# Two output blocks of the merged mixer formed in turn, and the retention heads' rows scaled and turned two heads at a time

## The chip, the cores and the metric

The kernel runs on one core of one Trainium2 chip. The metric is the device time of one execution in microseconds (us), as the median of several runs. The engines are named as in the profile: PE (TensorE, matmuls), PEld (its weight loads), DVE (VectorE), ACT (ScalarE), POOL (GpSimd) and SP (SyncE, which here issues DMAs). "L206" is line 206 of the kernel before.

## The reference

One decoder layer over S = 256 tokens of width D = 2048, all in float32, depth and batch 1. Shortened to what is computed:

```python
hn = rmsnorm(h, norm_mix_w)
q, k, v, g_ret, xr, yr, g_a, g_b = split(hn @ w_in)
q = rotary(q, positions); k = rotary(k, positions) * RET_QK_DIM ** -0.5
ret = head_groupnorm(chunkwise_retention(q, k, v), ret_gn_w)        # 8 heads, 256 wide each
ret_out = silu(g_ret) * ret
xr = causal_dwconv(xr, rnn_conv_w, rnn_conv_b)                      # 4 taps
rnn_out = gelu(yr) * rg_lru(xr, ...)
merged = sigmoid(g_a) * (ret_out @ w_proj_ret) + sigmoid(g_b) * (rnn_out @ w_proj_rnn)
h = h + merged @ w_mix_out
h = h + memory_cross_attention(rmsnorm(h), rmsnorm(mem), xa_w_q, xa_w_k, xa_w_v, xa_w_o)
h = h + conv_gated_ffn(rmsnorm(h), ffn_w_up, ffn_conv_w, ffn_conv_b, ffn_w_down)
return rmsnorm(h, final_norm_w)
```

## The kernel before

**Products.** A float32 product is made of three matmuls in a 32-bit format of lower precision (fp32r): each operand is split into a high part and the remainder, and high x high, low x high and high x low are added up in PSUM. All weights are read once. The host lays them out as a stream of chunks in the order of use; a chunk is 1 MB, four k-tiles of 128 rows by 512 columns. SP loads it into one of three raw buffers (L244), ScalarE makes its high parts (`hi`, L269), VectorE the remainders (`lo`, L270), two parts of two k-tiles each. There are six buffers for parts, three chunks' worth, and `prefetch` works two chunks ahead of the one that PE uses. A block of 512 output columns has 16 k-tiles, thus four chunks, and a chunk of the kind used here has 24 matmuls of 512 columns on PE (`mm`, L206; two token halves by four k-tiles by three products).

**Order.** `weight_plan` lists the blocks in the order in which the program takes them; `weight_stream` lists the chunks in the order in which they lie in memory, and an assertion holds the program to it. At the start, two blocks are already mixed chunk by chunk. At the end, three of the last blocks of `ffn_w_down` are streamed with the last chunk of each behind all the others. `steps_n` is a generator that does one chunk of a block at each step, and `ended` runs one to its end. The accumulators come from a PSUM pool of three. The order of instructions on each engine is fixed when the program is built: a scheduler places them by priorities and by its own estimate of times. Each engine then executes its list in order and waits where an operand isn't there yet.

**Work beside the products.** `later(n, fn)` puts a function off until n + 1 more chunks have been used. `by_dma(rows, then, wait)` turns a block of 256 token rows by 512 columns: ScalarE copies its two 16-bit halves into planes (`pl`, L380, two copies), SP issues two DMA transposes (L382, `pt`), and, put off by `wait`, ScalarE joins the halves again (`f`, L391, two copies) and `then` is called with the result.

**Places that matter here.**

- Retention: for a group of four heads, `normalise` (called when the fourth head's output is there) subtracts the mean and multiplies by the gate on VectorE, and scales by the inverse deviation on ScalarE (L653, eight instructions: four heads by two token halves) into two `rows` tiles of two heads each; both are then turned by `by_dma` with waits 2 and 3. The words go to the list `words`, which `split_head` uses ahead of `w_proj_ret`.
- Behind the second group come the RG-LRU blocks: products for `xr` and `yr`. `turned_rows` scales a product's rows (L404, VectorE) and turns them; `conv_x` then applies the conv, its first tap on ScalarE (L763) and three more for each of four tiles on VectorE (L765, 12 instructions).
- Merge: `gated` forms the gated block `m` (L806); block `b` of the merged activations is added up (L820) and turned by `by_dma` with the default wait of 1; `turn_merged` splits it into operands (`s`, L423 on ScalarE, L424 on VectorE).
- `residual("w_mix_out", ...)` takes the four blocks of `w_mix_out` one after the other. Each is added to the residual rows (`nat`, L835), squared for the norm (L850) and turned; `turn` splits it with the norm's weights (`split_cols`, L446 on ScalarE and L447 on VectorE). Before block 1, `memory_steps` squares the rows of the memory (L488, eight instructions); before block 3, it puts off the splits of the memory's pairs, which `xa_w_k` uses next.

Of the kernel before, what the change touches and what calls it, by code (L numbers as in the profile page):

```python
# [17 lines left out]
P = 128  # L18
D = 2048
S = 256  # L20
NT = D // P
HEADS = 8
DK = 128
DV = 256
# [4 lines left out]
BW = 512  # L29
KC = 4  # L30
# [37 lines left out]
def weight_plan():  # L68

    plan = []  # L70
    for g in range(2):
        for c in (O_Q, O_K):
            plan += [("w_in", 0, NT, c + g * BW), ("w_in", 0, NT, O_V + g * 1024 + (c == O_K) * BW)]
        plan += [("w_in", 0, NT, O_G + g * 1024 + b * BW) for b in range(2)]
    for b in range(4):
        plan += [("w_in", 0, NT, c + b * BW) for c in (O_XR, O_YR)]
    for c, w in ((O_GB, "w_proj_rnn"), (O_GA, "w_proj_ret")):
        for b in range(4):
            plan += [("w_in", 0, NT, c + b * BW), (w, 0, NT, b * BW)]
    plan += [("w_mix_out", 0, NT, b * BW) for b in range(4)]  # L80
    plan += [(w, 0, NT, b * BW) for b in range(4) for w in ("xa_w_k", "xa_w_q")]
    plan += [(w, 0, NT, b * BW) for w in ("xa_w_v", "xa_w_o") for b in range(4)]
    for kind, *a in ff_plan():
        if kind == "down":
            plan += [("ffn_w_down", a[0] * BW, 4 * a[1], b * BW) for b in range(4)]
        else:
            plan.append(("ffn_w_up", 0, NT, (0 if kind == "gate" else FF) + a[0] * BW))
    return plan
# [15 lines left out]
def pieces(i, nk):  # L104

    sizes = EARLY if i < 2 else [KC] * (nk // KC)
    return [(sum(sizes[:j]), n) for j, n in enumerate(sizes)]


def weight_stream():  # L110

    out = [
        [(w, row + k * P, n, c) for k, n in pieces(i, nk)]
        for i, (w, row, nk, c) in enumerate(weight_plan())
    ]
    out[:2] = [[one for pair in zip(*out[:2]) for one in pair]]
    out[-4:-1] = [[c for o in out[-4:-1] for c in o[:-1]] + [o[-1] for o in out[-4:-1]]]
    return [one for chunks in out for one in chunks]


# [10 lines left out]
def hybrid_layer(  # L131
# [16 lines left out]
    act, dve, pe, pool, sp = nc.scalar, nc.vector, nc.tensor, nc.gpsimd, nc.sync  # L148
# [11 lines left out]
    def nm(s):  # L160
        count[0] += 1
        return f"{s}_{count[0]}"

    def big(shape, dt=F32, s="b"):
        return bp.tile(shape, dt, tag="big", name=nm(s))
# [4 lines left out]
    def acc():  # L170
        return pm.tile([P, 2, BW], F32, tag="acc", name=nm("acc"))
# [108 lines left out]
    def later(n, fn):  # L280

        pending.append((step[0] + n + 1, fn))
# [18 lines left out]
    def ended(steps):  # L301

        for a in steps:
            pass
        return a
# [41 lines left out]
    def steps_n(w, row, st, nk, col):  # L347

        a = acc()
        for k0, n, parts in chunks(nk, w, row, col):  # L350
            for tt in range(2):
                for kk in range(n):
                    k = k0 + kk
                    hi, lo = (t[:, kk % KH, :] for t in parts[kk // KH])
                    products_n(a[:, tt, :], st[k // 2][:, k % 2, :], hi, lo, tt, k == 0, k == nk - 1)
                if tt == 0 and isinstance(st, Pairs):
                    st[min(NT, k0 + 3 * n) // 2 - 1]
            yield a

    def gemm_n(*args):  # L360
        return ended(steps_n(*args))
# [10 lines left out]
    def by_dma(rows, then, wait=1):  # L372


        planes = big([P, 2, 2, BW], U16, s="pl")
        turned_ = big([P, 2, 4, S], U16, s="pt")
        words = rows.bitcast(U16).rearrange("p t (n h) -> p h t n", h=2)
        with tc.high_priority(FREE):
            for h in range(2):
                act.copy(planes[:, :, h, :], words[:, h])  # L380
        for tt in range(2):
            sp.dma_start_transpose(  # L382
                out=turned_.rearrange("p h f s -> p (h f) s")[:, :, tt * P : (tt + 1) * P],
                in_=planes[:, tt].rearrange("p h n -> p (h n)"),
            )

        def join():
            f = big([P, 4, S], s="f")
            halves_ = f.bitcast(U16).rearrange("p f (s h) -> p h f s", h=2)
            for h in range(2):  # L390
                act.copy(halves_[:, h], turned_[:, h])  # L391
            then(f)

        later(wait, join)
# [97 lines left out]
    def sums():  # L492
        return sp_.tile([P, 2, 4], F32, tag="ss0", name=nm("ss"))
# [103 lines left out]
    ret, words = [], []  # L597
# [5 lines left out]
    def retain(g, qr, kr, vs, dec, gates):  # L603

        stats = sp_.tile([P, 8, 2], F32, tag="mv", name=nm("mv"))
        raws = []

        def scores(hh):
            sc = small((P, 384))
            k, q = kr[hh // 2], qr[hh // 2]  # L610
            product(sc[:, 0:S], halves(k, hh % 2, slice(0, P)), halves(q, hh % 2), True, True)
            late = slice(P, S)
            product(sc[:, S : S + P], halves(k, hh % 2, late), halves(q, hh % 2, late), True, True)
            pr_ = tp.tile([P, 384], F32, tag="pret", bufs=2, name=nm("pret"))
            dve.tensor_tensor(out=pr_[:, 0:S], in0=sc[:, 0:S], in1=dec[:, hh, :], op=ALU.mult)
            dve.tensor_tensor(out=pr_[:, S:384], in0=sc[:, S:384], in1=dec[:, hh, 0:P], op=ALU.mult)
            phi, plo = (tp.tile([P, 384], F32R, tag="tmp", name=nm("ps")) for _ in range(2))
            act.copy(phi, pr_)
            dve.tensor_tensor(out=plo, in0=pr_, in1=phi.bitcast(F32), op=ALU.subtract)
            later(0, lambda: values(hh, phi, plo))  # L620

        def values(hh, phi, plo):
            vc = slice((hh % 2) * DV, (hh % 2 + 1) * DV)
            v0, v1 = ([t[:, tt, vc] for t in vs[hh // 2]] for tt in range(2))
            p0, p1, p2 = ([t[:, c * P : (c + 1) * P] for t in (phi, plo)] for c in range(3))
            ro = small()
            product(ro[:, 0, :], p0, v0, True, True)
            product(ro[:, 1, :], p1, v0, True, False)
            product(ro[:, 1, :], p2, v1, False, True)
            bn = sp_.tile([P, 2, 6], F32, tag="bn", name=nm("bn"))  # L630
            rc = tmp("rc")
            act.copy(rc, ro)
            for tt in range(2):
                dve.bn_stats(out=bn[:, tt, :], in_=rc[:, tt, :])
                dve.bn_aggr(out=stats[:, 2 * hh + tt, :], in_=bn[:, tt, :])
            raws.append(rc)
            if hh == 3:
                normalise()

        def normalise():  # L640
            rows = [big([P, 2, BW], s="rows") for _ in range(2)]
            rstd = rsqrt_small(stats[:, :, 1], 8, 1.0, GN_EPS).rearrange("p (h t) -> p h t", t=2)
            for tt in range(2):
                dve.tensor_scalar_mul(rstd[:, :, tt], rstd[:, :, tt], rs0[:, tt : tt + 1])
            for hh in range(4):
                for tt in range(2):
                    y = raws[hh][:, tt, :]
                    dve.scalar_tensor_tensor(
                        out=y, in0=y, scalar=stats[:, 2 * hh + tt, 0:1],
                        in1=gates[hh // 2][:, tt, (hh % 2) * DV : (hh % 2 + 1) * DV],  # L650
                        op0=ALU.subtract, op1=ALU.mult,
                    )
                    act.mul(rows[hh // 2][:, tt, (hh % 2) * DV : (hh % 2 + 1) * DV], y, rstd[:, hh, tt : tt + 1])  # L653
            for i, r in enumerate(rows):
                by_dma(r, words.append, 2 + i)

        for hh in range(4):
            later(hh, lambda hh=hh: scores(hh))

    for g in range(2):  # L660
        dec = big([P, 4, S], s="dec")
        vs, turned = [], ([], [])
        for b, o in enumerate((O_Q, O_K)):
# [6 lines left out]
            if b == 1:  # L670
                sp.dma_start(
                    out=dec,
# [145 lines left out]
    for b in range(4):  # L818
        m = gated(O_GA, "w_proj_ret", ret, b, big([P, 2, BW], s="m"))
        dve.tensor_add(m, m, mb[b])  # L820
        by_dma(m, turn_merged)


    hrow = [load_rows(x, c) for c in range(4)]
# [3 lines left out]
    def residual(w, st, out, wcol, steps=None):  # L828

        ss = sums()  # L830
        for b in range(4):
            if steps:
                steps(b)
            h = hrow[b]
            dve.tensor_add(h, h, gemm_n(w, 0, st, NT, b * BW))  # L835
            squares(h, ss, b)
            by_dma(hrow[b], lambda f, b=b: turn(f, b, out, wcol))
        return ss
# [209 lines left out]
    for kind, b, *n in ff_plan():  # L1048
# [6 lines left out]
        else:  # L1055
            final = b + n[0] == NF // 4
            if final:
                wfin = []
                for i in range(2):
                    t = big([P, 2, BW], s="wf")  # L1060
                    sp.dma_start(
                        out=t.rearrange("p a n -> p (a n)"),
# [37 lines left out]
```

## Time and profile before

| what | value |
|---|---|
| median of three runs | 2025.03 us |
| the three runs | 2021.9, 2025.03, 2025.69 us |
| the profiled execution, its own time | 2022.28 us |
| its span from the first to the last instruction | 2020.5 us |
| mean granted clock of PE | 0.996 of full |
| instructions | 23630 |
| read from memory | 388.46 MB, 193 GB/s over the span |

The profile shows one execution. Its page gives for each engine the busy time, its share of the span and the number of instructions; groups of instructions by line, with the mean duration of one and what ended the idle time before them; and the chain of work that ended last. The waits list the idle time of an engine by line, with what it waited for: in all, times, longest. In a timeline, a line has start, duration, engine, line, operation, the tile written and those read, shapes and count, and in brackets the idle time before it and what ended that. In a table of windows, a line has the window and its length, then the busy time of PE, PEld, DVE, ACT and POOL with the instructions, then the clock granted to PE (PEclk, 1.00 is full speed), the busy share of the DMA engines and GB/s. Busy time of adjacent instructions overlaps a little, so that sums can exceed the window.

### The profile page before, as it was taken

What the parts mean: (1) busy time and instruction counts of PE and PEld (TensorE: products, weight loads), DVE (VectorE), ACT (ScalarE), POOL (GpSimd) and SP (SyncE); (2) the same over time, 40 slices, a digit from 0 to 9 for tenths busy, and PEclk for the clock granted to TensorE, in tenths of its full rate; (3) what the DMA queues carried; (4) which work ended last, traced back from release to release, by engine and by line L of the source; (5) the groups of instructions that cost most, each with busy time, mean ns of one, the idle gap of its engine ahead of it and who ended that gap; (6) DMA issues with size and microseconds to landing.
All of it is one profiled execution on the core that took longest, in us unless ns stands there. A gap on an engine that the chain in (4) does not pass through costs nothing.

```text
span 2020.5 us, 23630 instructions
## 1 busy us (share of the span) xinstructions
PE 2002.3 (99%) x9060; PEld 1666.2 (82%) x9060; DVE 1264.3 (63%) x1563; ACT 1246.0 (62%) x1502; POOL 7.7 (0%) x12
## 2 busy tenths in 40 slices
PE   9999999999999999999999999999999999999998
PEld 7888888888888888788888888888888888888887
DVE  5856756888645555456555554567675577664675
ACT  6546547989434555478666556666774566644763
POOL 0000000000000000000000000000000000000000
PEclk9999999999999999999999999999999999999999
DMA  8665656665555566777766546667666566655663
GB/s 304 225 210 173 234 199 192 228 213 188 208 188 190 197 204 214 259 225 242 219 198 204 182 167 208 209 189 218 228 203 232 193 195 214 227 215 198 210 228 125
DMA packets 185153, 421.99 MB, mean 209 GB/s; under 512 B 127440, under 2 KB 132176, under 8 KB 139984
## 3 DMA queue, kind: packets, MB, share of 16 engines
q1 hardware_dynamic: 183520, 417.85, 62.2%
q10 hardware_dynamic: 1520, 2.63, 0.4%
q8 instruction: 71, 1.16, 0.2%
q14 instruction: 42, 0.34, 0.1%
HBM read 388.46 MB, written 2.10 MB: 193 GB/s over the span
## 4 chain that ended last, share of the span: by engine, by line
PE 97%; ACT 1%; DVE 1%; DMA 1%; issue 1%; SPq 0%; POOL 0%; POOLq 0%; DVEq 0%; ACTq 0%
PE acc L206 94%; PE sm L206 3%; DMA raw<-in_wall 1%; DVE lo L270 0%; ACT f L391 0%; DVE xr L765 0%; ACT pl L380 0%; ACT rows L653 0%; ACT hi L269 0%; POOL ro L507 0%; PE sm L209 0%; SPq L244 0%; DVE s L447 0%; ACT nat L1034 0%; DVE rows L404 0%
## 5 line engine op out<-in xcount | busy, mean ns | idle before, releaser
L206 PE MATMUL acc<-hi,s 128*128 128x512 f32 (+1 forms) x5680 | 1741.6, 388 | 4.2 <-ACT s L423 4.0
L270 DVE TENSOR_TENSOR lo<-raw,hi 128x1024 fp32r<-128x1024 f32 (+1 forms) x714 | 861.1, 1220 | 662.4 <-ACT hi L269 636.5
L206 PEld LDWEIGHTS acc<-hi,s 128*128 128x128 f32 x5680 | 1062.5, 188 | 222.1 <-ACT s L423 4.5
L206 PE MATMUL acc<-lo,s 128*128 128x512 f32 (+1 forms) x2840 | 1100.8, 388 | 2.0 <-DVE lo L270 2.0
L269 ACT CAST hi<-raw 128x1024 fp32r<-128x1024 f32 (+1 forms) x712 | 736.0, 1051 | 535.4 <-PE acc L206 466.7
L206 PEld LDWEIGHTS acc<-lo,s 128*128 128x128 f32 x2840 | 533.7, 188 | 111.6 <-DVE lo L270 2.7
L391 ACT COPY f<-pt 128x1024 uint16<-128x1024 uint16 x114 | 146.5, 1350 | 68.8 <-DMA pt<-pl 68.6
L380 ACT COPY pl<-rows 128x1024 uint16<-128x1024 uint16 x90 | 89.8, 1046 | 66.1 <-DVE rows L404 58.2
L404 DVE TENSOR_SCALAR rows<-acc,ro 128x512 f32<-128x512 f32 x68 | 47.8, 747 | 2.4 <-PE acc L206 2.4
L957 DVE SCALAR_TENSOR_TENSOR fv<-f,pf,fv 128x255 f32<-128x255 f32 (+1 forms) x88 | 35.8, 479 | 0.7 <-ACT fv L955 0.7
L957 DVE SCALAR_TENSOR_TENSOR fg<-f,pf,fg 128x255 f32<-128x255 f32 (+1 forms) x88 | 35.6, 478 | 0.0
L955 ACT ACTIVATE fv<-f,pf 128x256 f32<-128x256 f32 x44 | 22.9, 596 | 0.0
L955 ACT ACTIVATE fg<-f,pf 128x256 f32<-128x256 f32 x44 | 22.9, 594 | 0.0
L423 ACT ACTIVATE s<-fo 128x512 fp32r<-128x512 f32 x22 | 13.6, 635 | 14.1 <-DVE fo L977 14.1
L380 ACT COPY pl<-nat 128x1024 uint16<-128x1024 uint16 x16 | 16.0, 1046 | 9.6 <-DVE nat L835 9.6
L765 DVE SCALAR_TENSOR_TENSOR xr<-f,pa,xr 128x255 f32<-128x255 f32 (+2 forms) x48 | 20.1, 481 | 2.1 <-ACT xr L763 2.0
L446 ACT ACTIVATE s<-f,pb 128x256 fp32r<-128x256 f32 x48 | 20.4, 501 | 0.0
L447 DVE SCALAR_TENSOR_TENSOR s<-f,pb,s 128x256 fp32r<-128x256 f32 x48 | 19.9, 480 | 0.0
L206 PEld LDWEIGHTS sm<-s,s 128*128 128x128 f32 x144 | 18.8, 191 | 0.9
L206 PE MATMUL acc<-s,hi 128*128 128x512 f32 x64 | 17.6, 413 | 1.0 <-DVE hi L267 1.0
L206 PE MATMUL sm<-s,s 128*128 128x256 f32 (+1 forms) x144 | 18.6, 279 | 0.0
L421 DVE TENSOR_TENSOR s<-f,s 128x512 fp32r<-128x512 f32 x16 | 10.3, 687 | 10.0 <-ACT s L420 10.0
(154 smaller groups left out, 630.0 us busy)
## 6 DMA issues: line engine op xcount, KB each, us to landing
raw<-in_wall SPq DMA_DIRECT2D x352, 1024.0 KB, 4.9
raw<-in_wall SPq DMA_DIRECT2D x6, 512.0 KB, 6.4
nat<-in_x ACTq DMA_DIRECT2D x4, 512.0 KB, 8.2
nat<-in_x SPq DMA_DIRECT2D x4, 512.0 KB, 5.7
nat<-in_mem SPq DMA_DIRECT2D x4, 512.0 KB, 9.0
xt<-in_mem_t SPq DMA_DIRECT2D x8, 256.0 KB, 3.7
pt<-pl SPq DMA_TRANSPOSE x114, 4.9
xt<-in_x_t SPq DMA_DIRECT2D x7, 256.0 KB, 6.3
```

Of the source, the lines that this page charges most:

```text
L206: tc.keep_in_program_order(pe.matmul(*a, **k))
L269: act.copy(hi[:, ds], raw[:, cs, :])
L270: dve.tensor_tensor(out=lo[:, ds], in0=raw[:, cs, :], in1=hi[:, ds].bitcast(F32), op=ALU.subtract)
L380: act.copy(planes[:, :, h, :], words[:, h])
L391: act.copy(halves_[:, h], turned_[:, h])
L404: dve.tensor_scalar_mul(rows[:, tt, :], a[:, tt, :], r[:, tt : tt + 1])
L423: act.mul(t[:, :, 0:S], src, scale)
L446: act.activation(t[:, j, 0:S], src[:, j, :], AF.Identity, scale=wcol(j))
L447: dve.scalar_tensor_tensor(out=t[:, j, S:BW], in0=src[:, j, :], scalar=wcol(j), in1=t[:, j, 0:S].bitcast(F32), op0=ALU.mult, op1=ALU.subtract,
L765: dve.scalar_tensor_tensor(out=y[:, s:S], in0=z[:, 0 : S - s], scalar=p_cw(3 - s, t), in1=y[:, s:S], op0=ALU.mult, op1=ALU.add,)
L955: act.activation(y, z[:, j, :], AF.Identity, scale=pf[:, 2, t : t + 1], bias=pf[:, 3, t : t + 1])
L957: dve.scalar_tensor_tensor(out=y[:, s:S], in0=z[:, j, 0 : S - s], scalar=pf[:, 2 - s, t : t + 1], in1=y[:, s:S], op0=ALU.mult, op1=ALU.add,)
```

## The change

Two things are changed.

1. A helper `in_turn` orders the chunks of several blocks so that the last chunk of each comes behind all the others. It takes the place of the expression that did this for `ffn_w_down`, and it is applied to the first two blocks of `w_mix_out` as well: the order becomes chunks 0 to 2 of block 0, chunks 0 to 2 of block 1, the last of block 0, the last of block 1, then blocks 2 and 3 as before. `residual` makes the four generators first and, where it is given steps (only for `w_mix_out`), advances the first two by three chunks each before it ends block 0. The merged block 3 is joined with a wait of 3 chunks, the others with 1 as before.
2. `normalise` no longer scales the rows of all four heads in one go. Subtraction and gate stay there; scaling and turning are done by `two_heads`, put off by `later(0, ...)` for heads 0 and 1 and by `later(1, ...)` for heads 2 and 3, each with a wait of 4 for the join.

No instruction is added or removed on any engine; their order changes.

```diff
+def in_turn(products):
+
+    return [c for o in products for c in o[:-1]] + [o[-1] for o in products]
...
     out[:2] = [[one for pair in zip(*out[:2]) for one in pair]]
-    out[-4:-1] = [[c for o in out[-4:-1] for c in o[:-1]] + [o[-1] for o in out[-4:-1]]]
+    out[-4:-1] = [in_turn(out[-4:-1])]
+    mix = [c[0][0] for c in out].index("w_mix_out")
+    out[mix : mix + 2] = [in_turn(out[mix : mix + 2])]
     return [one for chunks in out for one in chunks]
...
         def normalise():
-            rows = [big([P, 2, BW], s="rows") for _ in range(2)]
             rstd = rsqrt_small(stats[:, :, 1], 8, 1.0, GN_EPS).rearrange("p (h t) -> p h t", t=2)
...
-                    act.mul(rows[hh // 2][:, tt, (hh % 2) * DV : (hh % 2 + 1) * DV], y, rstd[:, hh, tt : tt + 1])
-            for i, r in enumerate(rows):
-                by_dma(r, words.append, 2 + i)
+
+            def two_heads(i):
+                rows = big([P, 2, BW], s="rows")
+                for hh in (2 * i, 2 * i + 1):
+                    for tt in range(2):
+                        c = (hh % 2) * DV
+                        act.mul(rows[:, tt, c : c + DV], raws[hh][:, tt, :], rstd[:, hh, tt : tt + 1])
+                by_dma(rows, words.append, 4)
+
+            for i in range(2):
+                later(i, lambda i=i: two_heads(i))
...
         dve.tensor_add(m, m, mb[b])
-        by_dma(m, turn_merged)
+        by_dma(m, turn_merged, 1 if b < 3 else 3)
...
         ss = sums()
+        products = [steps_n(w, 0, st, NT, b * BW) for b in range(4)]
         for b in range(4):
             if steps:
                 steps(b)
+                if b == 0:
+                    for one in products[:2]:
+                        for _ in range(NT // KC - 1):
+                            next(one)
             h = hrow[b]
-            dve.tensor_add(h, h, gemm_n(w, 0, st, NT, b * BW))
+            dve.tensor_add(h, h, ended(products[b]))
             squares(h, ss, b)
             by_dma(hrow[b], lambda f, b=b: turn(f, b, out, wcol))
```

## The prediction

> **What bounds the kernel.** The page's busy table comes first, then the waits of PE and the chain, last the timelines around PE's idle times.
>
> ```profile
> PE 2002.3 (99%) x9060; PEld 1666.2 (82%) x9060; DVE 1264.3 (63%) x1563; ACT 1246.0 (62%) x1502; POOL 7.7 (0%) x12
> ```
>
> TensorE (PE) does nothing else than its products for 99% of the span. The change alters no product and no byte, so it can only move PE's idle time and its clock. The waits of PE list that idle time:
>
> ```profile
> PE acc L206 <- ACT s L423: 4.0, 1, 4.0
> PE acc L206 <- DVE lo L270: 3.9, 5, 2.0
> ```
>
> One wait of 4.0 us is at the first w_mix_out block, and the longest wait for a remainder (lo), 2.0 us, is in an xr product behind the second retention group. The chain has the first, the timelines of VectorE and PE the second:
>
> ```profile
> 842.17 0.04 ACT hi L269
> ...
> 843.12 2.52 ACT f L391 x2
> ...
> 845.67 0.64 ACT s L423
> ...
> 846.35 84.08 PE acc L206 x359
> ```
>
> ```profile
> 336.27 2.85 DVE L765 SCALAR_TENSOR_TENSOR xr<-f,pa,xr 128x253 f32<-128x253 f32 x7
> 339.02 2.37 DVE L270 TENSOR_TENSOR lo<-raw,hi 128x1024 fp32r<-128x1024 f32 x2
> ```
>
> ```profile
> 340.31 0.50 PE L206 MATMUL acc<-lo,s 128*128 128x512 f32 x1 [1.98 <-DVE lo L270]
> ...
> 846.35 1.52 PE L206 MATMUL acc<-hi,s 128*128 128x512 f32 x2 [4.04 <-ACT s L423]
> ```
>
> At 842 PE has used merged blocks 0 to 2 and lacks block 3, whose join (f) sits on ScalarE behind a cast that itself waited for PE. At 338 the lo stands in VectorE's queue behind the conv's multiply-adds. An idle PE also costs clock; the windows show PEclk as the seventh value (after time and five engines), before, in and after the gaps:
>
> ```profile
> 338.40:340.30 1.90, 0.00 (x0) 0.00 (x0) 1.90 (x4) 1.90 (x3) 0.00 (x0) 1.00 0.01 1
> 844.00:844.50 0.50, 0.00 (x0) 0.00 (x0) 0.48 (x1) 0.50 (x2) 0.00 (x0) 0.78 1.03 401
> 846.40:848.90 2.50, 2.50 (x5) 1.73 (x6) 1.23 (x2) 0.42 (x1) 0.00 (x0) 0.50 1.07 394
> 851.00:851.50 0.50, 0.50 (x3) 0.37 (x2) 0.00 (x0) 0.00 (x0) 0.00 (x0) 0.89 1.03 426
> ```
>
> The clock halves at about 844.28 and is back at 851.11, 6.83 us later. With the only other pair (21.67 and 25.08, in the start) these times lie on one grid of 3.41 us: 844.28 - 25.08 is 240 steps of it. In the grid's window up to 844.28 PE had idled 1.97 us, in the one before 21.67 1.62 us; the gap at 338 falls into two windows, 0.83 and 1.15 us, and the clock stayed 1.00. So between 1.15 and 1.62 us idle in one window halves the clock in the next.
>
> **The gap at 842: a gain of 6.74 us.** Chunks take 5.44 us (casts at 819.00, 824.44, 829.88). Block 0 would have ended at 847.59 and ended at 854.33: 4.04 idle, the rest half clock. In turn, PE takes b0's chunks 0 to 2 to 842.15, b1's to 858.47, then b0's last, b1's last, and b2 from 869.35. Merged block 3, joined with wait 3 rather than 1, is ready at about 847.6, 11 us ahead of its first use; if that cover were gone, the gap would be back. Two open accumulators fit the pool of three, and the stream changes order, not size.
>
> **The gap at 338: a gain of 2.15 us.** The eight scalings (L653, 0.405 us each) and two pairs of plane copies (0.95 each) stood in one row on ScalarE and held up the join of xr and with it the conv. In the new order that join comes first, the scalings follow in two fours, one a chunk later. Replayed with these durations, the conv is on VectorE at 322 to 326.9, the chunk's first lo at 326.9 to 328.1 (needed at 332.6) and the next at 330.8 to 332.0 (needed at 338.1): 6 us of cover, 0 lost. The two pairs of transposes move with their copies on SP's queue; the raw loads behind them have no later issue than before. The first group (176 to 215 us) has 3 to 5 us of cover at each lo, before and after. The longer wait (4 for 2 and 3) gives the head's words later, but nothing uses them before w_proj_ret, hundreds of us on: nothing.
>
> **A new gap, at b2's third chunk: a loss of 3.4 us and of clock.** Before, the work of block 0's end and of the memory rows' squares lay in one spell between casts:
>
> ```profile
> 856.40 2.00 ACT L380 COPY pl<-nat 128x1024 uint16<-128x1024 uint16 x2 [1.04 <-DVE nat L835]
> 858.30 0.63 ACT L850 ACTIVATE junk<-nat 128x512 f32<-128x512 f32 x1
> ...
> 864.46 1.99 ACT L269 CAST hi<-raw 128x1024 fp32r<-128x1024 f32 x2
> 866.35 2.56 ACT L391 COPY f<-pt 128x1024 uint16<-128x1024 uint16 x2
> ...
> 869.72 1.71 ACT L446 ACTIVATE s<-f,pb 128x256 fp32r<-128x256 f32 x4
> ```
>
> Now block 1 ends one chunk behind block 0, so block 1's copies and splits enter the same row of ScalarE before the cast of b2's chunk 2 (due 880.23 on PE). Replayed in the new order: b0 ends at 863.91; its add to nat (L835) ends at 865.96; planes 866.0 to 867.9; ten squares (two of b0, eight of memory, 0.614 each) to 874.07; the join needs the transposes, issued at 868.03. Before, those issued at 858.42 took 5.3 and 5.7 each, the second begun 1.2 later, so 6.6 in all: 874.65. Join 2.43 to 877.1, a square 0.61, three splits 1.2, planes of block 1 1.9, the last split 0.4, a square 0.61: 881.8. Cast 1.05 and lo 1.2 to 884.1. PE needs that lo at its third matmul, 880.68. So it loses 884.1 - 880.68 = 3.4 us (about 0.6 of it crawling on what the hi allows, some 2.5 or more idle); if waiting at semaphores adds 0.03 to 0.1 at each of 15 steps or the transposes land 0.5 earlier, 2.9 to 4.8. The waiting cast holds up only the later casts, which have a chunk of cover. A gap of 2.5 falls on the grid so that one window holds over 1.62 in 78 of 100 positions; half speed for the rest of one window costs up to 1.7, two cost 2.5: I take 1.4, bounds 0 and 2.5.
>
> The Trainium skill, "TensorE: Matmul & The Clock Gate", section "HAM oscillation — how this bites in real kernels", has only idle gaps beyond some 3.4 us as harmful; by it this gap would keep its clock and the sum be 1.4 lower. The row 844.00 speaks against it: the clock went down 1.97 us into the gap.
>
> **Later.** Block 1's planes are transposed just behind block 0's, ahead of a raw load whose buffer is free only at 885.4: nothing. The splits of the memory pairs, shifted by a few us, end later at the third chunk of xa_w_k, which waited 0.39 already: 0.35 more, between 0 and 1.
>
> **Sum.** On the profiled execution: -2.15 - 6.74 + 3.4 + 1.4 + 0.35 = -3.74, so 2022.28 becomes 2018.5. That execution is 2.75 below the median 2025.03. Its gap at 338 was split by the grid 0.83 to 1.15; at 63 of 100 positions one part exceeds 1.62 and the clock halves, up to 1.7 more. This may be why the others are longer, and removing it is worth 1.1 on average. Against the median: -3.74 - 1.1 = -4.84, so 2020.2. That is 0.24%; 0.2% (4.05 us) is about what a measurement of this kernel can tell from no change, so the forecast lies at the border of "faster" (below 2020.98).
>
> **Rivals.**
> - *The new gap keeps full clock* (the skill's rule, above, or luck of the grid): 1.4 less, 2018.8. For: the gap at 338 kept it; against: the gaps before 21.67 and 844.28.
> - *No new gap.* ScalarE's row runs through in time, if the squares of memory go ahead of the wait for block 0 or the transposes land before 871: neither gap, 2020.2 - 3.4 - 1.4 = 2015.4. Against: in ScalarE's order block 0's planes, which wait for its add, stand ahead of those squares.
> - *The change doesn't do what it says at the retention heads*: the conv is in front of the lo as before, since the join still meets a busy ScalarE. Gap at 338 and its clock stay, 2020.2 + 2.15 + 1.1 = 2023.5.
> - *Slower: the transposes of b0 and b1 land late.* SP puts four transposes beside raw loads. Landing 6.6 us after issue gives the forecast; by 10.5 us the change is even, and beyond 12 it is slower by 0.2%. At 14.1 (12.8, as long as raw loads took between 828 and 845, plus 1.3 for the second) the join starts at 882.2: first gap 10.95, block 1's at b3's first chunk 4.7, clock 2 x 2.4, and 0.35: 20.8 against a gain of 6.74 + 2.15 + 1.1 = 9.99: 2035.8. Against: those loads stood behind eight 0.5 MB loads of rows that are not there at 866, and the longest time from issue to landing near is 8.0 (the pair at 880.39).
>
> **How the numbers follow.** Forecast 0.57 (own range 2018.3 to 2022.7: gap 2.9 to 4.8, clock 0 to 2.5; 0.31 faster, 0.25 same, 0.01 slower), full clock 0.13 (0.11 faster, 0.02 same), no new gap 0.10 (faster), heads unchanged 0.12 (0.11 same, 0.01 slower), late transposes 0.08 (slower). Faster 0.52, same 0.38, slower 0.10. The range 2015.0 to 2025.5 reaches from the third case to the fourth, with 2 us above it, half of the 3.8 by which the three runs of before differ; it leaves out the late transposes and little else.
>
> **What would show it.** Right: no wait of PE for an s of L423 (new L430) and none for a lo near 338; the conv's multiply-adds end near 327; a wait of some 2.5 us for a lo of b2's third chunk, 881 to 884, PEclk near 0.5 behind it. Wrong: PE idle before b0's last chunk, a lo waiting behind conv work, the join (L398) of block 0 starting later than 877, or no gap at 881.

## The result, and the profile after

The changed kernel takes 2018.26 us (median of nine runs, 2016.84 to 2020.61). Nine runs of the kernel before have a median of 2022.92 (2021.9 to 2025.69). The ratio is 0.9977, with a 95% interval of 0.9968 to 0.9986: 4.66 us less at the medians (by the interval 2.8 to 6.5), where 4.84 was forecast. The profiled execution took 2020.61 us, the longest of the nine, with a span of 2018.8.

The page's busy table, and PE's waits in the changed kernel (columns: waiting engine, tile and line, what it waited for, then us in total, times, longest):

```profile
PE 2004.0 (99%) x9060; PEld 1667.2 (83%) x9060; DVE 1264.3 (63%) x1563; ACT 1242.9 (62%) x1502; POOL 7.7 (0%) x12
```

```profile
PE acc L213 <- ACT hi L276: 3.1, 1, 3.1
PE acc L213 <- DVE lo L277: 2.7, 2, 1.9
```

The 4.0 us wait for an s is gone. A wait of 3.1 us for a cast (hi) has come. Of the two waits for a lo, 1.9 us lies in the start and 0.8 at 1510 us; none is near 338. PE's busy time grew by 1.7 us although its instructions are the same. In the stretches that are named below, it grew by 0.7 in the start, 0.5 in *mix* and 0.8 in *FFN* and fell by 0.3 at *heads*, so the half clock behind the new gap explains little of it. On the timeline of ScalarE in the changed kernel, the join of xr now stands ahead of the scalings (L665); on VectorE's, all 12 of the conv's instructions run in one piece and the lo behind them is early:

```profile
317.82 2.57 ACT L398 COPY f<-pt 128x1024 uint16<-128x1024 uint16 x2 [2.87 <-DMA pt<-pl]
...
323.18 1.69 ACT L665 ACTIVATE rows<-rc,ro 128x256 f32<-128x256 f32 x4
```

```profile
322.48 4.80 DVE L779 SCALAR_TENSOR_TENSOR xr<-f,pa,xr 128x255 f32<-128x255 f32 x12
327.20 1.22 DVE L277 TENSOR_TENSOR lo<-raw,hi 128x1024 fp32r<-128x1024 f32 x1
```

The new gap is at b2's third chunk. The chain of the changed kernel leads there through block 0's transposes and then link by link along ScalarE's row:

```profile
866.64 5.59 DMA pt<-pl
...
873.80 1.33 ACT f L398
...
875.72 1.20 ACT s L453 x3
876.92 1.88 ACT pl L387 x2
878.80 0.41 ACT s L453
879.21 0.61 ACT junk L869 x2
879.82 0.94 ACT hi L276
880.77 0.04 issue
880.81 1.22 PE acc L213 x2
```

PE had run dry at 877.72 and resumes at 880.81, when the cast that all this stands in front of is done. The windows of the changed kernel show what the clock did (PEclk is the value ahead of the last two):

```profile
879.50:880.00 0.50, 0.00 (x0) 0.00 (x0) 0.23 (x1) 0.50 (x3) 0.00 (x0) 1.00 0.00 0
880.00:880.50 0.50, 0.00 (x0) 0.00 (x0) 0.00 (x0) 0.50 (x1) 0.00 (x0) 0.92 1.00 201
880.50:881.00 0.50, 0.19 (x1) 0.19 (x2) 0.21 (x1) 0.50 (x2) 0.00 (x0) 0.50 1.13 206
884.00:884.50 0.50, 0.50 (x3) 0.40 (x2) 0.50 (x2) 0.50 (x1) 0.00 (x0) 0.50 0.55 66
887.00:887.50 0.50, 0.50 (x3) 0.45 (x2) 0.50 (x1) 0.50 (x2) 0.00 (x0) 0.76 0.84 344
```

It fell at 880.42 and came back at 887.24, two steps of 3.41 us later.

A profile differs from the next by a few us in places that the change doesn't touch. So the profiles are compared by stretches of PE, each from one named product to another: *heads* from the second retention group's last product to the first RG-LRU gate products (313.66 to 344.23 in the kernel before), *mix* from there to the first logits of the cross-attention (985.46), and *FFN* from the feed-forward's first product to the end of the span (from 1211.86). What lies between retention's start and its end, and the cross-attention from its first logits on, agree within 0.02 us in all profiles. The start takes 47.3 to 49.9 us, by chance. All profiles of this study are in the table; the medians are of nine runs (before, changed), eleven (e1, e2), six (e7) or five (e3, e4, e8); e5, e6, e9 and f1 to f3 were run once, for the profile. The kernel before, run beside e1 to e4 and beside e7 and e8, had medians of 2022.82 and 2022.97.

| kernel | heads, us | mix, us | FFN, us | median us |
|---|---|---|---|---|
| before | 30.57 | 641.23 | 808.64 | 2022.92 |
| before, again (f1) | 30.54 | 641.15 | 809.66 | |
| changed | 28.30 | 640.68 | 810.16 | 2018.26 |
| mix-out only (e1) | 32.15 | 637.51 | 809.25 | 2020.41 |
| mix-out only, again (f3) | 30.54 | 638.07 | 811.24 | |
| heads only (e2) | 28.30 | 642.54 | 811.94 | 2021.59 |
| heads only, again (f2) | 28.30 | 642.33 | 810.96 | |
| changed, joins late (e3) | 28.30 | 634.99 | 810.42 | 2015.02 |
| changed, squares early (e4) | 28.31 | 635.86 | 811.29 | 2015.44 |
| before, heads' words joined late (e5) | 30.54 | 641.27 | 809.86 | |
| before, heads split, old waits (e6) | 28.30 | 641.92 | 811.22 | |
| mix-out only, joins late (e7) | 30.54 | 635.35 | 809.85 | 2016.20 |
| changed, all three edits (e8) | 28.30 | 634.08 | 810.08 | 2012.93 |
| changed, merged block 3 joined with wait 1 (e9) | 28.30 | 640.64 | 811.35 | |

In the profiled pair, the span fell by only 1.7 us: start 0.39 less, heads 2.27 less, mix 0.55 less, FFN 1.52 more.

### The profile page after: what moved, and what is told of

The parts are those of the page before. It is cut to its first block, busy times and chain, and to the rows that moved or that the text cites. A ratio compares the mean times of both kernels' runs of the same rounds, so it can differ in the third digit from the quotient of the medians.

```text
span 2018.8 us, 23625 instructions
## 1 busy us (share of the span) xinstructions
PE 2004.0 (99%) x9060; PEld 1667.2 (83%) x9060; DVE 1264.3 (63%) x1563; ACT 1242.9 (62%) x1502; POOL 7.7 (0%) x12
## 3 DMA queue, kind: packets, MB, share of 16 engines
q8 instruction: 71, 1.16, 0.2%
## 4 chain that ended last, share of the span: by engine, by line
PE 91%; ACT 2%; DVE 2%; DMA 2%; issue 2%; SPq 0%; POOLq 0%; POOL 0%; ACTq 0%; DVEq 0%
PE acc L213 88%; PE sm L213 3%; DMA pt<-pl 2%; ACT hi L276 1%; DVE lo L277 1%; DMA raw<-in_wall 1%; ACT pl L387 1%; ACT f L398 0%; DVE fv L976 0%; DVE rows L411 0%; ACT fg L974 0%; DVE s L431 0%; DVE fg L976 0%; SPq L389 0%; DVE fo L996 0%
## 5 line engine op out<-in xcount | busy, mean ns | idle before, releaser
L213 PE MATMUL acc<-hi,s 128*128 128x512 f32 (+1 forms) x5680 | 1741.5, 388 | 3.1 <-ACT hi L276 3.1
L213 PEld LDWEIGHTS acc<-hi,s 128*128 128x128 f32 x5680 | 1062.7, 188 | 219.9 <-ACT hi L276 3.9
L213 PE MATMUL acc<-lo,s 128*128 128x512 f32 (+1 forms) x2840 | 1101.5, 388 | 0.8 <-DVE lo L277 0.8
L213 PEld LDWEIGHTS acc<-lo,s 128*128 128x128 f32 x2840 | 533.9, 188 | 112.5 <-DVE lo L277 3.3
L454 DVE SCALAR_TENSOR_TENSOR s<-f,pb,s 128x256 fp32r<-128x256 f32 x48 | 20.0, 478 | 6.1 <-ACT s L453 6.1
L213 PEld LDWEIGHTS sm<-s,s 128*128 128x128 f32 x144 | 18.8, 191 | 0.9
L213 PE MATMUL sm<-s,s 128*128 128x256 f32 (+1 forms) x144 | 18.6, 279 | 0.0
L213 PE MATMUL acc<-s,hi 128*128 128x512 f32 x64 | 17.4, 407 | 0.0
```

The source lines that it names most:

```text
L213: tc.keep_in_program_order(pe.matmul(*a, **k))
L454: dve.scalar_tensor_tensor(out=t[:, j, S:BW], in0=src[:, j, :], scalar=wcol(j), in1=t[:, j, 0:S].bitcast(F32), op0=ALU.mult, op1=ALU.subtract,
```

## The experiments

Theory: the heads' part removes the gap at 338; the mix-out part removes the one at 842 and makes a new one at b2's third chunk out of ScalarE's row, which gives most of it back. Rivals: the mix-out part carries the gain alone; or the new gap is due to the raw loads behind the transposes.

**e1, the mix-out part alone.** The retention heads as before:

```diff
-            for i in range(2):
-                later(i, lambda i=i: two_heads(i))
+            for i, r in enumerate(rows):
+                by_dma(r, words.append, 2 + i)
```

> Only the mix-out part: w_mix_out's first two blocks in turn, merged block 3 joined with wait 3; the retention heads as before. Theory: the 4.0 us gap before b0's last chunk goes (with its clock, 6.74 us), the new gap at b2's third chunk comes (3.1 us idle and about 3.2 us of half clock in the changed kernel's profile), and the wait of 2.0 us for a lo near 338 us stays; net 0.4 to 1.5 us less than before, about 2022. Rival: the mix-out part carries the gain and the gap at 338 costs next to nothing in most runs: about 2018.5.

Median 2020.41, ratio 0.9990 (0.9981 to 0.9999): 2.4 us less than before, more than the 0.4 to 1.5 expected and between the two theories. The gaps are where the theory has them. From PE's timeline of this kernel:

```profile
338.32 0.50 PE L213 MATMUL acc<-lo,s 128*128 128x512 f32 x1 [1.94 <-DVE lo L277]
...
882.34 0.73 PE L213 MATMUL acc<-hi,s 128*128 128x512 f32 x2 [2.33 <-ACT hi L276]
```

The clocks are the other way round from the earlier profiles. Windows of e1:

```profile
339.00:339.50 0.50, 0.50 (x3) 0.39 (x2) 0.50 (x2) 0.50 (x1) 0.00 (x0) 0.66 1.12 199
...
880.00:882.30 2.30, 0.01 (x1) 0.00 (x0) 0.48 (x1) 2.30 (x6) 0.00 (x0) 1.00 0.35 68
```

Here the clock fell after the gap at 338 (heads 32.15 rather than 30.54) and held through the new one (mix 637.51 rather than 640.68). I had put the new gap's price at what one profile showed; the price depends on where the gap falls on the clock's grid.

**e2, the heads' part alone.** The kernel before with the new `normalise`.

> Only the retention part: rows scaled and turned two heads at a time, joins with wait 4; mix-out as before. Theory: the wait for a lo near 338 us is gone, the 4.0 us wait for s near 840 stays, no gap near 880; 2.2 us less, and up to 1.7 more where the clock dropped after that gap: 2.3 to 3.9 less than before, about 2019.5. Rival (mix-out carries the gain): within 1 us of before, about 2022.

Median 2021.59, ratio 0.9995 (0.9987 to 1.0004): 1.2 us less, and less than the 2.3 to 3.9 expected. The interval runs from 2.6 us less to 0.8 more, so the runs alone exclude neither 2.3 nor the rival's value. At the medians, neither half has the whole gain of 4.7 us (2.4 and 1.2); what each does is settled by the stretches, not by the medians. The stretch itself does what was said, 28.30, without a wait; the 4.0 us wait for s is as before (`PE acc L206 <- ACT s L423: 4.0, 1, 4.0` in its waits). What the rest of the run did with the 2.24 us comes below (f1 to f3).

**e3, joins of mix-out blocks 0 and 1 put off.** On the changed kernel:

```diff
-            by_dma(hrow[b], lambda f, b=b: turn(f, b, out, wcol))
+            by_dma(hrow[b], lambda f, b=b: turn(f, b, out, wcol), 3 if steps and b < 2 else 1)
```

> The changed kernel, with the joins of mix-out blocks 0 and 1 put off by 3 chunks rather than 1, so that the casts of b2's third chunk stand ahead of them on ScalarE (planes of b0 863.3 to 865.2, five squares, planes of b1 to about 870.2, seven squares to 874.5, cast to 875.5, due 877.56). Theory: no gap at b2's third chunk, 6.3 us less than the changed kernel, about 2012. Rival 1 (the gap comes from the raw load, held up on SP by the four transposes, and not from ScalarE's row): the gap stays or moves to b3's first chunk, about 2016 to 2018. Rival 2 (the half clock behind the gap costs less than it seems): 3.1 less, about 2015.

The gap is gone and the stretch *mix* is 634.99, 5.7 us less than in the changed kernel: the 6.6 us of the new gap and its clock, less 0.9 that PE now loses in `xa_w_k`. ScalarE's timeline in e3, and PE's window over the place:

```profile
868.34 1.98 ACT L387 COPY pl<-nat 128x1024 uint16<-128x1024 uint16 x2
...
874.53 3.88 ACT L276 CAST hi<-raw 128x1024 fp32r<-128x1024 f32 x4
878.32 2.56 ACT L398 COPY f<-pt 128x1024 uint16<-128x1024 uint16 x2
```

```profile
874.00:882.00 8.00, 8.00 (x37) 6.64 (x36) 4.82 (x5) 8.00 (x11) 0.57 (x1) 1.00 0.48 147
```

The casts start at 874.53, as worked out, ahead of the join; PE is busy for all 8 us at full clock. The raw loads were not the cause. The median, 2015.02 (ratio 0.9964, 0.9950 to 0.9978), is 3.2 us below the changed kernel's; 6.3 was expected from the one profile, 3.1 if the clock didn't count. The changed kernel's profile was one in which the clock had fallen; a gap with the clock held costs 3.4 (e1 against e8).

**e4, the memory's squares early.** On the changed kernel:

```diff
-        if b == 1:
+        if b == 0:
             ss = sums()
-            for c in range(4):
-                sum_squares(mnat[c], ss, c)
-            rsms.append(rstd_rows(ss))
+
+            def rows_of(c):
+                sum_squares(mnat[c], ss, c)
+                if c == 3:
+                    rsms.append(rstd_rows(ss))
+
+            for c in range(4):
+                later(2 + c, lambda c=c: rows_of(c))
```

> The changed kernel, with the memory rows' eight squares spread over four chunks from b0's third on, so that they leave ScalarE's row behind block 0; the joins stay, but the cast of b2's third chunk then stands ahead of the join of block 0. Theory: no gap at b2's third chunk; block 1's planes still come late (876 to 878), and the raw load queued behind their transposes may hold b3's first chunk by 0 to 2 us: 4 to 6.3 less than the changed kernel, 2012 to 2014.5. Rival (transposes landing late are what holds the row, squares cost nothing): the gap stays, about 2018.

No gap at b2's third chunk; mix is 635.86, and the median 2015.44 (0.9965, 0.9952 to 0.9977), 2.8 us below the changed kernel. The rival falls, though it has half a point: the join still starts when the transposes land (871.41, behind 0.41 us of waiting), but the casts no longer stand behind it. The feared wait at b3's first chunk did not come; instead PE waits 1.3 us for a split of the memory's pairs (`PE acc L213 <- DVE s L454: 1.3, 1, 1.3`).

**e5 and e6, which half of the heads' edit counts.** e5 is the kernel before with longer waits only, e6 the new `normalise` with a shorter wait:

```diff
 # e5
-                by_dma(r, words.append, 2 + i)
+                by_dma(r, words.append, 4 + i)
 # e6
-                by_dma(rows, words.append, 4)
+                by_dma(rows, words.append, 2)
```

> The kernel before with one edit: the joins of the retention heads' words wait 4 and 5 chunks rather than 2 and 3; the eight scalings stay in one row. Looked at: the stretch of PE from the second group's last retention product (313.66 in before) to the first RG-LRU gate products (344.23): 30.57 us before, 28.30 in the changed kernel. Theory (the row of scalings, waiting 4.07 us for the inverse deviation, stands in front of the join of xr): the gap stays, 30.3 to 32.3. Rival (the words' joins fill ScalarE and delay its casts): the gap goes, 28.3.

> The kernel before with the scalings and turns two heads at a time, and the joins put off by 2 chunks rather than 4 (so that they come at the times of before or one chunk later). The same stretch: theory (it is the place of the scalings behind the join of xr that counts, not the longer wait): 28.3, no wait of PE. Rival (the longer wait is needed as well): over 29.

The stretch *heads* took 30.54 us in e5 and 28.30 in e6: the order of the scalings decides, the waits do nothing. ScalarE's timelines, e5 first, then e6:

```profile
319.19 2.11 ACT L653 ACTIVATE rows<-rc,ro 128x256 f32<-128x256 f32 x5 [4.06 <-DVE ro L644]
...
328.08 2.57 ACT L391 COPY f<-pt 128x1024 uint16<-128x1024 uint16 x2
```

```profile
317.08 2.55 ACT L391 COPY f<-pt 128x1024 uint16<-128x1024 uint16 x2 [2.52 <-DMA pt<-pl]
...
322.43 1.70 ACT L658 ACTIVATE rows<-rc,ro 128x256 f32<-128x256 f32 x4
```

In e5, ScalarE stands idle for 4.06 us in front of the first scaling, which waits for the inverse deviation (ro), and the join of xr comes some 10 us later than in e6, where it starts as soon as its data have landed. The idle time is not the whole of it: behind it come the eight scalings (3.2 us), the two pairs of plane copies (3.8) and two casts, all ahead of the join.

**e7, e3 without the heads' part.**

> The mix-out part with the joins of blocks 0 and 1 put off by 3 chunks, the retention heads as before: the kernel of e3 without the retention part. Theory: the gap at 338 is the only difference to e3: 2.3 us more, and up to 1.7 more where the clock drops after it: 2.3 to 3.9 more than e3 (2015.0), 2017.3 to 2018.9. Rival (the retention part is worth no more than the 1.2 us by which e2's median lay below before's): 2016.2 or less.

Median 2016.20 (0.9969, 0.9957 to 0.9981), 1.2 us above e3 and below the 2017.3 to 2018.9 expected, again at the rival's value, although the stretch is 2.24 us longer (30.54 against 28.30) and mix 0.36. This profile's start was 1.8 us shorter than e3's and its FFN stretch 0.6 us; of the medians only the difference is known, and with six runs of 2014.79 to 2017.26 against five of 2013.81 to 2017.5 it does not tell 1.2 from 2.6.

**e8, all three edits.** e3 and e4 together, and six of the memory's pairs split during b3 instead of four:

```diff
-            for k2 in range(4):
-                later(k2, lambda k2=k2: ms[k2])
+            for k2 in range(6):
+                later(k2 // 2, lambda k2=k2: ms[k2])
```

> The changed kernel with all three: joins of mix-out blocks 0 and 1 put off by 3 chunks, the memory rows' squares spread over four chunks from b0's third on, and six of the memory's pairs split during b3 instead of four. Theory: no wait of PE in mix-out and none (0.6 us in e3, 1.3 in e4) at xa_w_k's third chunk; the stretch from the first gate products to the first products of the cross-attention is 634.2 us against 635.0 in e3; the median 0.5 to 1 us below e3, about 2014.3. Rival: more splits in b3 delay b3's casts, a new wait there, at or above e3's 2015.0.

Mix is 634.08, PE waits for nothing in the stretches heads and mix, and the median is 2012.93 (0.9953, 0.9940 to 0.9965): the best of all kernels here, 5.3 us below the changed one and 10.0 below before. The stretch is as expected (634.2); the median lies 2.1 below e3's, where 0.5 to 1 was expected.

**e9, merged block 3 with the common wait.**

```diff
-        by_dma(m, turn_merged, 1 if b < 3 else 3)
+        by_dma(m, turn_merged)
```

> The changed kernel with merged block 3 joined with a wait of 1 chunk like the others. Theory: the order of the chunks alone gives block 3 its cover, and ScalarE's order is the same: no wait of PE before b0's last chunk; the new gap at b2's third chunk stays, 2.3 to 3.1 us idle, and the stretch from the first gate products to the cross-attention is 637.5 (clock kept) to 640.7 (clock down over two windows). Rival (the longer wait of the join is part of the gain): a wait of PE for a cast or a lo between 825 and 850.

Mix 640.64 and no wait between 825 and 850: the order of the chunks gives the cover, the longer wait nothing. The new gap was 3.00 us and the clock fell for two windows.

**f1 to f3, the rest of the run.** The heads' part gained 1.2 us at the median twice where its stretch gained 2.24, a difference that lies within the noise of both medians. Up to then, the FFN stretch had been longer in each of the seven kernels with the heads changed than in the four without, though its instructions and their order on PE, ScalarE and VectorE are the same. The buffers in which its tiles lie can be others; the profile does not name them.

> The kernel before, profiled once more. Looked at: the stretch from the feed-forward's first product to the end, whose instructions and their order are the same in all kernels here. So far 808.6 to 809.9 us in the four with the retention heads as before, 810.1 to 811.9 in the seven with the heads changed. Theory (the heads' change costs about 1.5 us there, by an effect that reaches it through the buffers in which its tiles lie): below 810. Rival (chance of the transposes' landing times): anywhere from 808.6 to 812.

> The retention part alone, profiled once more, for the same stretch. Theory (the heads' change costs there): above 810. Rival (chance): anywhere from 808.6 to 812. The stretch at 338 again 28.3 us, the wait of 4.0 us for s near 840 again there, with the clock down for one or two windows of 3.41 us behind it.

> The mix-out part alone, profiled once more, for the same stretch. Theory (the heads' change costs there, the mix-out part does not): below 810. Rival (chance): anywhere from 808.6 to 812. The stretch from the first gate products to the cross-attention 637.5 us if the clock holds through the gap at b2's third chunk, 640.7 if it is down for two windows.

f1 and f2 fell as the theory had it (809.66, 810.96), f3 did not (811.24 with the heads as before). So the two groups overlap; their means are 809.75 (six profiles) and 810.93 (eight). What makes the differences inside is seen: transposes land at different times, and a late join passes its delay down the feed-forward's row until PE waits for a lo. At one place, 562 us into the stretch, PE loses 0.1 to 0.9 us in the five profiles in which a join some 30 us ahead of it came 7.0 to 7.8 us behind its plane copies (f3, e2, e4, e6, e9), and nothing in the nine in which it came after 6.1 to 6.8. In the changed kernel's profile the last link is

```profile
1510.93 0.50 PE L213 MATMUL acc<-lo,s 128*128 128x512 f32 x1 [0.77 <-DVE lo L277]
```

At two other places, 257 and 285 us into the stretch, each of the eight profiles with the heads changed loses 0.1 to 0.8 us against the fastest, and of the six others only e7 does (0.1). This speaks for some effect of the heads' edit, of 0.5 us in the mean there; how it would get there is not shown. Whether the edit moves the mean of the whole stretch by some 1.2 us or whether this is chance stays open.

## Why the prediction was right, point by point

**The gap at 842, 6.74 us: right.** It is absent in every kernel with the new chunk order. Mix is 641.23 before and 634.08 in e8, 7.15 less; by the starts of PE's matmuls, 6.74 of that is lost at this gap and 0.41 in `xa_w_k`. That is the execution from which the forecast was made; the other five profiles of the old order lose 6.4 to 7.4 at the gap, by where it falls on the clock's grid.

**The gap at 338, 2.15 us: right, measured 2.24,** and for the reason given. One thing was missed on the way: the 4.06 us for which ScalarE waited in front of the scalings are part of the row's price, beside the scalings and plane copies that I named. The conv was forecast at 322 to 326.9 and ran from 322.48 to 327.28, in a profile whose start was 0.39 us shorter.

**The clock after that gap, 1.1 us on average: mis-sized.** It fell in one (e1) of the six profiles that have the gap, not in 63 of 100; 1.6 us in one of six is 0.27. The step that failed is the threshold: 1.62 us of idle in one window came from the start, where the products have another shape; in mid-kernel, 1.83 to 1.87 left the clock up (below). With 1.9 in its place, some 45 of 100 positions would bring the clock down, an estimate from the gap of 1.95 and the grid of 3.41 us; whether one of six is fewer than that or chance, six profiles can't tell. The term's other ground was that before's three runs had a median 2.75 above the profiled execution; with nine runs it is 0.64 above.

**The new gap, 3.4 us: right in place, cause and size.** By the replay the join starts at 874.65 and the cast at 881.8, on before's clock; less the 2.67 us by which PE was earlier at that point, 871.98 and 879.13; measured 872.59 and 879.73. PE lost 3.43 us there in e1 where the clock held (637.51 against 634.08), 3.8 in f3. The detail was off: PE waited for the cast itself, at the chunk's first product, and hardly for the lo.

**Its clock, 1.4 us with bounds 0 and 2.5: mis-sized in the single case.** Where it fell (the changed kernel, e9), it was down for 6.8 us, and mix was 6.6 us above e8 in all, so 3.2 for the clock; where it held (e1, f3), 0. I had let the clock return after one window; it needed two, since PE resumed only 0.39 us after the fall and that little was enough to keep it low. Over the four profiles its mean is 1.6, beside the 1.4 taken; as the single price was 3.2 or nothing, the agreement of the mean is luck. Their mix stretch lies 5.1 us above e8's on average, where the forecast's terms make 5.5 (3.4, 1.4, and 0.39 and 0.35 for the wait in `xa_w_k`).

**Later, 0.35 more at `xa_w_k`: wrong, also in its sign.** The changed kernel, e9 and e1 lose nothing there and f3 0.2, where the six profiles of the old order lose 0.4 to 1.1, 0.75 on average. That PE comes there later, behind the new gap, is a likely reason; no run shows it.

By the rule of the Trainium skill that only gaps beyond some 3.4 us are harmful ("TensorE: Matmul & The Clock Gate", section "HAM oscillation — how this bites in real kernels"), the new gap would never have cost clock. The gaps of 3.09 (changed) and 3.00 us (e9) did; the traces decide against the rule here.

**The sum.** At the medians, -4.84 was forecast and -4.66 measured. That they agree so closely is partly luck: errors of the parts cancel. On the averages of the table, heads fell by 2.5 (30.81 to 28.30), where 2.15 and 1.1 make 3.25, too much by the clock at 338. Mix fell by 2.5 (641.74 in the six profiles of the old order to 639.23 in the four with the new gap), where the forecast's terms make 1.6; the largest part of that error is the term for `xa_w_k`. What the FFN stretch gave back, if anything, is open. The profiled pair, for which -3.74 was forecast, shows -1.67: its mix, with the clock down for two windows, came out 1.0 dearer than forecast and its FFN 1.5 longer, its start 0.4 shorter.

**The rivals.** Full clock in the new gap happens (e1, f3), by its place on the grid. "No new gap" and "heads unchanged" did not happen. Late transposes: the last of block 0's took 5.59 us from issue, near the 5.3 to 5.7 assumed.

## What to carry to other kernels

Moving an operand's last use behind other work removes a wait, but it also brings the ends of two blocks together, and their small steps on a helper engine then stand in one row ahead of the next cast: replay that row before the move, and put off the steps that nobody waits for (here two joins, 3.2 us at the median, with no other edit). In a row of instructions in order, look for one that waits for a late scalar in front of one whose data are there: the others pay for the idle time before it (here 4.06 us) as well as for its own duration. A gap on PE costs its length plus a clock that depends on chance, so one profile's price for it is one draw.

## What the runs showed of the hardware

The clock's changes lie on a grid of 3.41 us in every profile, and its two directions have different thresholds. Idle time of PE in one window, among products of 512 columns in mid-kernel, that left the clock up: up to 1.87 us (e1, new gap), 1.85 (e7, at 338) and 1.83 (e5, at 842). Idle time that brought it down at the window's end: 1.94 (e1, at 338), 1.97 (before), and from 2.4 to a whole window in e5, f1, e9, changed, f2, e2 and e6. Near products of 256 columns in the start, less was enough: 1.62 (before) and 1.78 (e3) brought it down, 1.43 (e1) did not, so idle time alone does not fix the threshold. Once down, the clock stayed down after windows with 0.35 (e9), 0.39 (changed), 0.55 (e6), 0.80 (e2), 1.16 (f2) and 2.07 us (before) of idle and came back after windows with none. f1 shows the cheapest form: the gap at 842 ended well inside a window, and the whole next one was busy, so one window at half speed was all:

```profile
844.00:845.00 1.00, 0.78 (x3) 0.41 (x4) 1.00 (x2) 0.38 (x1) 0.00 (x0) 1.00 1.06 389
845.00:846.00 1.00, 1.00 (x4) 0.81 (x3) 0.18 (x1) 0.00 (x0) 0.00 (x0) 0.50 1.05 387
848.00:849.00 1.00, 1.00 (x5) 0.82 (x4) 0.00 (x0) 0.00 (x0) 0.00 (x0) 0.79 0.99 410
```

So the same gap of 4.0 us at 842 cost from 6.4 (f1, e5, one window) to 7.4 us (e6, two windows; PE's starts against e8's), by chance of its place. Matmuls' ends are modelled in the profile, so the threshold between 1.87 and 1.94 is known no better than that.
